# A feed-forward slab of two chunks, with its second products between the next slab's first products

## The chip, the cores and the metric

The kernel runs on one core of a Trainium2 chip. The metric is the device time of one execution in microseconds. A profile of one execution gives the span from the first to the last instruction and what each engine did in it: TensorE (PE for matmuls, PEld for loading their weights), VectorE (DVE), ScalarE (ACT), GpSimd (POOL) and SyncE (SP), which issues nearly all transfers from memory.

## The reference

The kernel computes one decoder layer in float32 on 256 tokens of 2048 channels: a SwiGLU feed-forward part, a token mixer, a second feed-forward part and a last normalization.

```
def swiglu(h, w_in, w_out):
    gu = h @ w_in
    gate, up = gu[..., :D_FF], gu[..., D_FF:]
    return (jax.nn.silu(gate) * up) @ w_out

# h = h + 1/2 * SwiGLU_1(RMSNorm(h))
# u = RMSNorm(h) @ W_in_mix, pooling heads and gated linear attention on parts of u
# h = h + concat(y_pool, y_gla) @ W_out_mix
# h = h + 1/2 * SwiGLU_2(RMSNorm(h))
# output = RMSNorm_final(h)
```

D_FF is 5632, so that a feed-forward part multiplies 256 x 2048 by 2048 x 11264 (the first product, gate and up) and 256 x 5632 by 5632 x 2048 (the second product).

## The kernel before, in words

**Numbers.** Each float32 operand is split into a rounded part hi and a remainder lo, and a product is three matmuls of 128x512: hi by hi, hi by lo, lo by hi (`three`, L165). Weights arrive raw, 1 MB a step (`load`, L101, three buffers). ScalarE writes hi (L108), VectorE writes lo (L109), into tiles of 128x1024 from a pool `units` of 14.

**Steps.** A step multiplies a 2 x 2 block of activations (two token tiles, two channel tiles of 128) by a 2 x 2 block of weights (two channel tiles, two column blocks of 512). In kind S that is 8 products (24 matmuls, `Group.s`). In kind W it is 7 (21 matmuls, `Group.w`), in the manner of Winograd: VectorE makes differences of weight blocks (`w_step`, L147, L151, L153), their splits follow, and the activations come with four sums S1 to S4 (`s_sums`, L342, split like the rest). Two of the results of W steps gather in tiles of their own (pw) and are put together by `combine` (L271 on ScalarE, L272 to L275 on VectorE); the result goes to the other accumulators by L428 in a first product and to h by L473 in a second product.

**Stages.** The first product goes in 11 chunks of 512 columns of gate and up, 8 steps each. A chunk of kind PLAIN has 8 S steps, one of MIXED 4 S and 4 W steps. After a chunk ScalarE takes silu (L435), VectorE multiplies by up (fa, L437), TensorE transposes (ftp, L444, eight of 128x128), and hi and lo of the result (fhi L449, flo L450) are the activations of the second product. Chunks are gathered in slabs of 4, 4 and 3. When the chunks of a slab are done, its second product runs in two halves of 1024 output columns, with 8 or 6 steps (table OUT), and is added to h with a factor 0.5 (`to_h`, L473; in the last slab of the first feed-forward part `finish1`, L592, which goes on to the transposes tp_h and splits h_hi, h_lo, L290, that the mixer needs). Names: fi and zi are first products of the first and second part, fo and zo second products; fo8_0 is half 0 of the slab that begins with chunk 8; wl_fo1_19 is a lo tile of half 1, step 19.

**Order.** The program is written as one list; a scheduler sets the order on each engine from it, and each engine runs its own list in order. x comes transposed in pairs of channel tiles (`x_act`, L530), is scaled and split within chunk 0, and for four of the eight pairs the sums S1 to S4 are made at the same place. The tiles for them, for fa and for raw x come from a pool `tmp` with two buffers of tag "act". Accumulators and pw tiles use two groups of PSUM banks, x and y, that change places with each product.

## Time and profile before

| | |
|---|---|
| median of 3 runs | 1734.99 us (1734.27 to 1735.23) |
| the profiled execution | 1734.83 us |
| its span | 1733.1 us |
| granted TensorE clock, mean over the span | 0.997 |
| busy share: TensorE, VectorE, ScalarE | 99%, 76%, 53% |
| read from memory | 334.56 MB, 194 GB/s over the span |

Times in the profile are in microseconds from the span's start unless marked ns. A matmul's duration in a list is longer than its pace, since matmuls overlap; the pace is read from starts, or from how long a row of them takes in the chain of waits. In the same way instructions of one engine that follow each other overlap by a little: a row "x4" of a timeline runs from the first's start to the last's end. A bracket "[0.77 <-DVE wl_fo L109]" is the time that the engine was idle before the row, and who ended it. What lies around the span in the profiled execution is 1.7 us.

### The profile page before, as it was taken

How to read it: one execution, taken by the hardware profiler on the slowest of the kernel's cores; microseconds unless marked ns; L12 is line 12 of the kernel's file. 1: busy time of each engine (PE TensorE's matmuls, PEld its weight loads, DVE VectorE, ACT ScalarE, POOL GpSimd, SP SyncE). 2: the span in 40 equal slices, each digit the busy share in tenths (PEclk: the TensorE clock that was granted, in tenths of full speed). 3: DMA queues.
4: the chain of work that ended last, by engine and by line, in shares of the span. 5: the costliest groups of instructions: out<-in, count | busy, mean ns of one | idle time of the engine just before them, and what ended most of it. 6: DMA issues, size and time to landing. Idle time of an engine off the chain costs nothing.

```text
span 1733.1 us, 20485 instructions
## 1 busy us (share of the span) xinstructions
PE 1717.8 (99%) x7840; PEld 1427.4 (82%) x7840; DVE 1316.3 (76%) x1493; ACT 911.1 (53%) x1117; POOL 24.9 (1%) x23
## 2 busy tenths in 40 slices
...
GB/s 344 189 230 169 194 235 194 189 199 187 201 210 182 215 196 148 211 183 140 200 212 146 191 176 168 224 165 194 201 236 167 222 165 200 217 219 150 252 189 91
DMA packets 52340, 337.98 MB, mean 195 GB/s; under 512 B 6017, under 2 KB 9217, under 8 KB 13330
## 3 DMA queue, kind: packets, MB, share of 16 engines
...
q8 instruction: 61, 1.00, 0.2%
...
HBM read 334.56 MB, written 2.10 MB: 194 GB/s over the span
## 4 chain that ended last, share of the span: by engine, by line
PE 97%; DMA 1%; ACT 1%; DVE 1%; issue 0%; SPq 0%; DVEq 0%; POOLq 0%; POOL 0%; ACTq 0%
PE ps_zi L165 24%; PE ps_fi L165 22%; PE ps_fo L165 11%; PE ps_zo L165 11%; PE ps_h L165 5%; PE pw_fi L165 3%; PE pw_zi L165 3%; PE ps_mp L165 3%; PE ps_mv L165 3%; PE pw_fo L165 2%; PE pw_zo L165 2%; PE ps_mg L165 2%; PE ps_mq L165 1%; PE ps_mk L165 1%; PE ps_mgr L165 1%; PE ftp L444 1%
## 5 line engine op out<-in xcount | busy, mean ns | idle before, releaser
L109 DVE TENSOR_TENSOR wl_zi<-wr_zi,wh_zi 128x1024 fp32r<-128x1024 f32 (+1 forms) x216 | 250.3, 1173 | 104.7 <-ACT wh_zi L108 98.1
L108 ACT CAST wh_zi<-wr_zi 128x1024 fp32r<-128x1024 f32 (+1 forms) x216 | 215.6, 1013 | 213.5 <-PE ps_zi L165 142.0
L109 DVE TENSOR_TENSOR wl_fi<-wr_fi,wh_fi 128x1024 fp32r<-128x1024 f32 (+1 forms) x218 | 249.8, 1163 | 85.7 <-ACT wh_fi L108 81.4
L108 ACT CAST wh_fi<-wr_fi 128x1024 fp32r<-128x1024 f32 (+1 forms) x218 | 214.4, 1004 | 189.5 <-PE ps_fi L165 116.5
L165 PE MATMUL ps_fi<-wh_fi,xT_hi 128*128 128x512 f32 x584 | 227.4, 391 | 1.7 <-ACT wh_fi L108 1.7
L165 PE MATMUL ps_fi<-wl_fi,xT_hi 128*128 128x512 f32 x584 | 228.4, 391 | 0.0
L165 PE MATMUL ps_zi<-wl_zi,h_hi 128*128 128x512 f32 x584 | 228.0, 390 | 0.0
L165 PE MATMUL ps_zi<-wh_zi,h_hi 128*128 128x512 f32 x584 | 227.9, 390 | 0.0
L165 PE MATMUL ps_zi<-wh_zi,h_lo 128*128 128x512 f32 x584 | 227.7, 390 | 0.0
L165 PE MATMUL ps_fi<-wh_fi,xT_lo 128*128 128x512 f32 x584 | 227.1, 391 | 0.1
L108 ACT CAST wh_zo<-wr_zo 128x1024 fp32r<-128x1024 f32 (+1 forms) x116 | 111.1, 999 | 96.9 <-DMA wr_zo<-in_ffn_w_out 34.0
L108 ACT CAST wh_fo<-wr_fo 128x1024 fp32r<-128x1024 f32 (+1 forms) x116 | 111.4, 999 | 94.4 <-DMA wr_fo<-in_ffn_w_out 34.8
L109 DVE TENSOR_TENSOR wl_fo<-wr_fo,wh_fo 128x1024 fp32r<-128x1024 f32 (+1 forms) x116 | 130.1, 1156 | 33.4 <-ACT wh_fo L108 33.1
L109 DVE TENSOR_TENSOR wl_zo<-wr_zo,wh_zo 128x1024 fp32r<-128x1024 f32 (+1 forms) x116 | 131.5, 1169 | 31.3 <-ACT wh_zo L108 30.9
L165 PEld LDWEIGHTS ps_fi<-wh_fi,xT_hi 128*128 128x128 f32 x584 | 110.0, 188 | 25.1 <-ACT wh_fi L108 2.6
L165 PEld LDWEIGHTS ps_fi<-wl_fi,xT_hi 128*128 128x128 f32 x584 | 110.1, 189 | 23.0 <-DVE wl_fi L109 0.4
L165 PEld LDWEIGHTS ps_fi<-wh_fi,xT_lo 128*128 128x128 f32 x584 | 109.9, 188 | 23.1 <-DVE xT_lo L290 0.5
L165 PEld LDWEIGHTS ps_zi<-wh_zi,h_lo 128*128 128x128 f32 x584 | 109.7, 188 | 22.5
L165 PEld LDWEIGHTS ps_zi<-wh_zi,h_hi 128*128 128x128 f32 x584 | 109.6, 188 | 22.4
L165 PEld LDWEIGHTS ps_zi<-wl_zi,h_hi 128*128 128x128 f32 x584 | 109.7, 188 | 22.3
L165 PE MATMUL ps_fo<-wl_fo,fhi 128*128 128x512 f32 x268 | 104.8, 391 | 0.8 <-DVE wl_fo L109 0.8
L165 PE MATMUL ps_zo<-wl_zo,zhi 128*128 128x512 f32 (+1 forms) x272 | 105.2, 387 | 0.0
...
## 6 DMA issues: line engine op xcount, KB each, us to landing
wr_zi<-in_ffn_w_in SPq DMA_DIRECT2D x88, 1024.0 KB, 5.0
wr_fi<-in_ffn_w_in SPq DMA_DIRECT2D x86, 1024.0 KB, 5.0
wr_fo<-in_ffn_w_out SPq DMA_DIRECT2D x44, 1024.0 KB, 5.0
wr_zo<-in_ffn_w_out SPq DMA_DIRECT2D x44, 1024.0 KB, 5.1
wr_h<-in_w_out_mix SPq DMA_DIRECT2D x16, 1024.0 KB, 4.9
wr_mv<-in_w_mv SPq DMA_DIRECT2D x8, 1024.0 KB, 4.8
wr_mp<-in_w_mp SPq DMA_DIRECT2D x8, 1024.0 KB, 4.9
...
```

What stands on the lines that cost most here:

```text
L108: nc.scalar.copy(out=hi, in_=src)
L109: nc.vector.tensor_tensor(out=lo, in0=src, in1=hi.bitcast(F32), op=ALU.subtract)
L165: nc.tensor.matmul(ps, x, y, start=start and i == 0, stop=stop and i == 2, **kw)
L444: nc.tensor.transpose(tp[:, t, k, :], a_t[t][:, k * P : (k + 1) * P], ident)
```

## The change

Slabs are of two chunks, the last of three. The second product of a slab is no longer behind its chunks: its half 0 stands behind the first chunk of the next slab, its half 1 behind the second. Only the last slab's second product stands at the end. The kinds of steps are listed by chunk: no W step in chunk 0, two in chunk 1, three in chunk 2, four in each of chunks 3 to 10; second products have S steps alone, but for two W steps in half 1 of the last slab. x is scaled and split in chunk 0 as before, but its sums S1 to S4 are made after chunk 0, from four pairs that are loaded again (`x_sums`). The tiles of the second product's activation sums go from three buffers to two. The loops of `ffn` become the functions `first_product` and `second_product`, called in the order of GROUPS.

```diff
-SLABS = ((0, 1, 2, 3), (4, 5, 6, 7), (8, 9, 10))
+SLABS = ((0, 1), (2, 3), (4, 5), (6, 7), (8, 9, 10))
...
-PLAIN = "SSSSSSSS"
-MIXED = "SWSWSWWS"
-MIXED_CHUNKS = (1, 3, 5, 7, 9)
+KINDS = (
+    "SSSSSSSS", "SSWSWSSS", "SSWSWWSS", "SWSWWWSS", "SWSWWWSS", "SWSWWWSS", "SWSWWWSS", "SWSWWWSS",
+    "SWSWWWSS", "SWSWWWSS", "SWSWWWSS",
+)
...
-    4: (
-        ((0, 0, "S"), (0, 1, "S"), (1, 0, "W"), (2, 0, "S"), (1, 1, "W"), (3, 0, "S"), (2, 1, "W"), (3, 1, "S")),
-        ((0, 0, "S"), (0, 1, "S"), (2, 0, "S"), (1, 0, "W"), (3, 0, "S"), (1, 1, "W"), (2, 1, "S"), (3, 1, "S")),
+    2: (
+        ((0, 0, "S"), (0, 1, "S"), (1, 0, "S"), (1, 1, "S")),
+        ((0, 0, "S"), (0, 1, "S"), (1, 0, "S"), (1, 1, "S")),
     ),
     3: (
-        ((0, 0, "S"), (0, 1, "S"), (1, 0, "W"), (2, 0, "S"), (1, 1, "W"), (2, 1, "S")),
+        ((0, 0, "S"), (0, 1, "S"), (1, 0, "S"), (1, 1, "S"), (2, 0, "S"), (2, 1, "S")),
         ((0, 0, "S"), (0, 1, "S"), (1, 0, "W"), (1, 1, "W"), (2, 0, "S"), (2, 1, "S")),
     ),
...
+GROUPS = (0, 1)
+for _s in range(1, len(SLABS)):
+    GROUPS += (SLABS[_s][0], (_s - 1, 0), SLABS[_s][1], (_s - 1, 1), *SLABS[_s][2:])
+GROUPS += ((len(SLABS) - 1, 0), (len(SLABS) - 1, 1))
...
+        for g in GROUPS:
+            if isinstance(g, int):
+                first_product(g)
+                continue
+            slab, ending = SLABS[g[0]], g[0] == len(SLABS) - 1
+            if ending and g[1] == 0 and behind is not None:
                 behind()
...
+            second_product(slab, g[1], ending)
...
-                if kp in W_PAIRS:
-                    nc.scalar.activation(out=f[:, j, :], in_=f[:, j, :], func=AF.Copy, scale=col)
-                else:
-                    scaled_split(hi[:, j, :], lo[:, j, :], f[:, j, :], col)
+                scaled_split(hi[:, j, :], lo[:, j, :], f[:, j, :], cols[j])
                 xT[2 * kp + j] = hi[:, j, :], lo[:, j, :]
-            if kp in W_PAIRS:
-                split_to(hi, lo, f)
-                x_s[kp] = s_factors(spool1, f, kp, "x")
         return xT[kt]
+
+    def x_sums():
+        for kp in W_PAIRS:
+            f, cols = x_pair(kp, "xs")
+            for j in range(2):
+                nc.scalar.activation(out=f[:, j, :], in_=f[:, j, :], func=AF.Copy, scale=cols[j])
+            x_s[kp] = s_factors(spool1, f, kp, "x")
```

In the kernel after, the lines named above have other numbers: L109 is L116, L147 L154, L151 L158, L153 L160, L272 to L275 L279 to L282, L165 L172, L428 L437, L437 L446, L444 L453, L473 L483, L592 L614, L342 L349, L290 L297.

VectorE at the end of a second product, in the first feed-forward part, before: half 1 of the first slab (fo0_1) and the splits of the next first product's plain chunk (fi4) around it.

```order
L272 TENSOR_TENSOR add_fo0_1_1_2092<-pw_fo0_1_0_1992,add_fo0_1_0_2091 128x512
L109 TENSOR_TENSOR wl_fi4_1_0_2209<-wr_fi4_1_2206,wh_fi4_1_0_2208 128x1024
L273 TENSOR_TENSOR add_fo0_1_0_2091<-pw_fo0_1_1_1993,add_fo0_1_1_2092 128x512
L274 TENSOR_TENSOR add_fo0_1_1_2092<-pw_fo0_1_1_1993,add_fo0_1_1_2092 128x512
L473 SCALAR_TENSOR_TENSOR h0_76<-add_fo0_1_0_2091,h0_76 128x1024
L109 TENSOR_TENSOR wl_fi4_1_1_2213<-wr_fi4_1_2206,wh_fi4_1_1_2212 128x1024
L275 TENSOR_TENSOR add_fo0_1_1_2092<-pw_fo0_1_1_1993,add_fo0_1_1_2092 128x512
L109 TENSOR_TENSOR wl_fi4_2_0_2243<-wr_fi4_2_2240,wh_fi4_2_0_2242 128x1024
L473 SCALAR_TENSOR_TENSOR h1_77<-add_fo0_1_1_2092,h1_77 128x1024
L473 SCALAR_TENSOR_TENSOR h0_76<-ps_fo0_1_0_1867,h0_76 128x1024
L473 SCALAR_TENSOR_TENSOR h1_77<-ps_fo0_1_1_1868,h1_77 128x1024
```

The same place after, at the end of half 0 of the second slab (fo2_0), with the splits of chunk 5 (fi5), whose pairs 1, 3, 4 and 6 are W steps.

```order
L116 TENSOR_TENSOR wl_fi5_3_0_2435<-wr_fi5_3_2432,wh_fi5_3_0_2434 128x512
L154 TENSOR_TENSOR wr_fi5_3_2432<-wr_fi5_3_2432 128x1024
L116 TENSOR_TENSOR wl_fi5_1_3_2372<-wr_fi5_1_2354,wh_fi5_1_3_2371 128x1024
L483 SCALAR_TENSOR_TENSOR h0_76<-ps_fo2_0_0_2178,h0_76 128x1024
L483 SCALAR_TENSOR_TENSOR h1_77<-ps_fo2_0_1_2179,h1_77 128x1024
L116 TENSOR_TENSOR wl_fi5_2_0_2401<-wr_fi5_2_2398,wh_fi5_2_0_2400 128x1024
L116 TENSOR_TENSOR wl_fi5_2_1_2405<-wr_fi5_2_2398,wh_fi5_2_1_2404 128x1024
L116 TENSOR_TENSOR wl_fi5_3_1_2439<-wr_fi5_3_2432,wh_fi5_3_1_2438 128x1024
L158 TENSOR_TENSOR wr_fi5_3_2432<-wr_fi5_3_2432 128x512
L160 TENSOR_TENSOR wr_fi5_3_2432<-wr_fi5_3_2432 128x512
L116 TENSOR_TENSOR wl_fi5_3_2_2445<-wr_fi5_3_2432,wh_fi5_3_2_2444 128x1024
L116 TENSOR_TENSOR wl_fi5_3_3_2450<-wr_fi5_3_2432,wh_fi5_3_3_2449 128x1024
```

The combine of a second product and two of its four additions to h are gone; two additions stand among the splits and differences of a W chunk, and this comes eight times in a feed-forward part where it came four times.

TensorE in chunk 1 before: where the transposes of chunk 0's result (ftp0) stand.

```order
L165 MATMUL ps_fi1_1_547<-wh_fi1_0_1_554,xT_lo0_113 128x512
L444 MATMUL ftp0_531<-ident_80,fa0_0_525 128x128 x4
L165 MATMUL ps_fi1_1_547<-wh_fi1_0_1_554,xT_hi0_109 128x512
...
L165 MATMUL ps_fi1_0_546<-wh_fi1_2_0_628,xT_hi1_110 128x512
L444 MATMUL ftp0_531<-ident_80,fa0_1_529 128x128 x4
L165 MATMUL pw_fi1_0_603<-wh_fi1_1_0_584,xT_hi0_109 128x512
```

The same after, in chunk 1 still, but behind the first matmuls of the second W step (pair 3).

```order
L172 MATMUL ps_fi1_0_562<-wh_fi1_3_1_716,shi_x_3_509 128x512
L172 MATMUL ps_fi1_0_562<-wl_fi1_3_1_717,shi_x_3_509 128x512
L172 MATMUL ps_fi1_0_562<-wh_fi1_3_1_716,slo_x_3_510 128x512
L453 MATMUL ftp0_547<-ident_80,fa0_0_541 128x128 x4
L172 MATMUL ps_fi1_1_563<-wh_fi1_3_3_727,xT_hi1_110 128x512
...
L453 MATMUL ftp0_547<-ident_80,fa0_1_545 128x128 x4
L172 MATMUL pw_fi1_0_653<-wh_fi1_1_0_634,xT_hi0_109 128x512
```

The transposes moved from a place in chunk 1's first step to one in its fifth.

VectorE at the end of the first feed-forward part's half 0 of the last slab (fo8_0) before, with the splits for half 1 (fo1).

```order
L273 TENSOR_TENSOR add_fo8_0_0_5237<-pw_fo8_0_1_5139,add_fo8_0_1_5238 128x512
L274 TENSOR_TENSOR add_fo8_0_1_5238<-pw_fo8_0_1_5139,add_fo8_0_1_5238 128x512
L151 TENSOR_TENSOR wr_fo1_18_5398<-wr_fo1_18_5398 128x512
L147 TENSOR_TENSOR wr_fo1_19_5442<-wr_fo1_19_5442 128x1024
L473 SCALAR_TENSOR_TENSOR h0_76<-add_fo8_0_0_5237,h0_76 128x1024
L109 TENSOR_TENSOR wl_fo1_18_2_5411<-wr_fo1_18_5398,wh_fo1_18_2_5410 128x1024
L275 TENSOR_TENSOR add_fo8_0_1_5238<-pw_fo8_0_1_5139,add_fo8_0_1_5238 128x512
L153 TENSOR_TENSOR wr_fo1_18_5398<-wr_fo1_18_5398 128x512
L592 SCALAR_TENSOR_TENSOR h0_76<-ps_fo8_0_0_5047,h0_76 128x512 x2
L473 SCALAR_TENSOR_TENSOR h1_77<-add_fo8_0_1_5238,h1_77 128x1024
L109 TENSOR_TENSOR wl_fo1_18_3_5416<-wr_fo1_18_5398,wh_fo1_18_3_5415 128x1024
L592 SCALAR_TENSOR_TENSOR h1_77<-ps_fo8_0_1_5048,h1_77 128x512 x2
```

The same place after.

```order
L154 TENSOR_TENSOR wr_fo1_19_5448<-wr_fo1_19_5448 128x1024
L116 TENSOR_TENSOR wl_fo1_18_1_5411<-wr_fo1_18_5404,wh_fo1_18_1_5410 128x1024
L158 TENSOR_TENSOR wr_fo1_18_5404<-wr_fo1_18_5404 128x512
L160 TENSOR_TENSOR wr_fo1_18_5404<-wr_fo1_18_5404 128x512
L614 SCALAR_TENSOR_TENSOR h0_76<-ps_fo8_0_0_5080,h0_76 128x512 x2
L614 SCALAR_TENSOR_TENSOR h1_77<-ps_fo8_0_1_5081,h1_77 128x512 x2
L116 TENSOR_TENSOR wl_fo1_18_2_5417<-wr_fo1_18_5404,wh_fo1_18_2_5416 128x1024
L116 TENSOR_TENSOR wl_fo1_18_3_5422<-wr_fo1_18_5404,wh_fo1_18_3_5421 128x1024
L116 TENSOR_TENSOR wl_fo1_19_1_5455<-wr_fo1_19_5448,wh_fo1_19_1_5454 128x1024
```

The combine of half 0 and its two additions L473 are gone from between the splits; the four L592, now L614, stand together.

## Rows read from the trace of the kernel before

**Rows 1.** The page: busy time of each engine with its share of the span and its instructions, and the shares of the chain that ended last by engine.

```profile
PE 1717.8 (99%) x7840; PEld 1427.4 (82%) x7840; DVE 1316.3 (76%) x1493; ACT 911.1 (53%) x1117; POOL 24.9 (1%) x23
...
PE 97%; DMA 1%; ACT 1%; DVE 1%; issue 0%; SPq 0%; DVEq 0%; POOLq 0%; POOL 0%; ACTq 0%
```

**Rows 2.** The waits of TensorE: what waited for what, us in total, times, the longest.

```profile
PE ps_fi L165 <- ACT wh_fi L108: 1.7, 1, 1.7
PE idle L519 <- DVE zeros L516: 1.2, 1, 1.2
PE ps_fo L165 <- DVE wl_fo L109: 0.8, 1, 0.8
PE ps_mgr L165 <- ACT h_hi L289: 0.4, 1, 0.4
PE ps_fo L165 <- ACT wh_fo L108: 0.4, 1, 0.4
PE ps_mgr L165 <- DVE h_lo L290: 0.2, 1, 0.2
```

**Rows 3.** The chain that ended last, three pieces of it: start, us, what.

```profile
36.86 20.47 PE ps_fi L165 x89
...
265.13 46.92 PE ps_fi L165 x207
...
329.34 7.48 PE ps_fi L165 x33
```

**Rows 4.** Stretches of the span: from and to, their length, then busy time and instructions of PE, PEld, DVE, ACT and POOL, the granted TensorE clock, the share of DMA, GB/s. They are the start, 10 us around the end of chunk 0, a plain chunk (4), a mixed chunk (5), both halves of the second slab's second product, and the place of the waits in Rows 2 at a second product (the end of the first feed-forward part).

```profile
0.00:11.00 11.00, 8.14 (x21) 4.36 (x22) 4.18 (x10) 5.44 (x10) 0.69 (x6) 0.87 0.76 237
...
50.00:60.00 10.00, 10.00 (x48) 8.26 (x47) 9.30 (x11) 7.85 (x9) 0.00 (x0) 1.00 0.39 117
...
265.10:308.30 43.20, 43.20 (x193) 35.76 (x192) 26.44 (x24) 18.34 (x20) 0.00 (x0) 1.00 0.52 179
308.30:350.30 42.00, 42.00 (x191) 34.77 (x190) 34.77 (x37) 23.87 (x27) 0.00 (x0) 1.00 0.60 216
436.60:521.20 84.60, 84.60 (x379) 70.10 (x378) 75.50 (x78) 43.89 (x48) 0.00 (x0) 1.00 0.57 201
690.00:705.00 15.00, 13.88 (x67) 10.94 (x67) 13.61 (x18) 10.54 (x21) 0.00 (x0) 1.00 0.42 130
```

**Rows 5.** TensorE in the order of time, 698 to 702 us: start, us to the end, what, and the idle time before it.

```profile
698.02 0.39 PE L165 MATMUL ps_fo<-wh_fo,fsolo 128*128 128x512 f32 x1
698.76 0.49 PE L165 MATMUL ps_fo<-wh_fo,fhi 128*128 128x512 f32 x1 [0.35 <-ACT wh_fo L108]
700.02 0.50 PE L165 MATMUL ps_fo<-wl_fo,fhi 128*128 128x512 f32 x1 [0.77 <-DVE wl_fo L109]
...
701.05 1.03 PE L370 MATMUL tp_h<-ident,h 128*128 128x128 f32 x8
701.94 0.50 PE L165 MATMUL ps_fo<-wl_fo,fhi 128*128 128x512 f32 x1
```

**Rows 6.** VectorE in the order of time, ahead of that place.

```profile
679.43 0.68 DVE L272 TENSOR_TENSOR add_fo<-pw_fo,add_fo 128x512 f32<-128x512 f32 x1
...
684.70 1.22 DVE L473 SCALAR_TENSOR_TENSOR h<-add_fo,h 128x1024 f32<-128x1024 f32 x1
685.84 1.22 DVE L109 TENSOR_TENSOR wl_fo<-wr_fo,wh_fo 128x1024 fp32r<-128x1024 f32 x1
...
688.17 1.28 DVE L592 SCALAR_TENSOR_TENSOR h<-ps_fo,h 128x512 f32<-128x512 f32 x2
...
698.74 1.22 DVE L109 TENSOR_TENSOR wl_fo<-wr_fo,wh_fo 128x1024 fp32r<-128x1024 f32 x1 [0.45 <-ACT wh_fo L108]
```

**Rows 7.** TensorE in the order of time in chunk 0.

```profile
36.35 0.39 PE L165 MATMUL ps_fi<-wl_fi,xT_hi 128*128 128x512 f32 x1
36.86 0.50 PE L165 MATMUL ps_fi<-wh_fi,xT_lo 128*128 128x512 f32 x1
```

**Rows 8.** The page's transfers: issuer, number, KB each, median us from issue to landing (the weights of first products, and the pairs of x).

```profile
wr_fi<-in_ffn_w_in SPq DMA_DIRECT2D x86, 1024.0 KB, 5.0
...
xr<-in_xT SPq DMA_DIRECT2D x8, 256.0 KB, 6.9
```

**Rows 9.** VectorE's groups by line and shape, 265.13 to 521.21 us (the second slab's four chunks and its second product): instructions, busy us and mean ns of one, idle time before them and who ended it.

```profile
L109 DVE TENSOR_TENSOR wl_fi<-wr_fi,wh_fi 128x1024 fp32r<-128x1024 f32 x72 | 87.1, 1223 | 35.9 <-ACT wh_fi L108 34.1 <-PE ps_fi L165 1.2
...
L437 DVE SCALAR_TENSOR_TENSOR fa<-ps_fi,rx_r,fs 128x512 f32<-128x512 f32 x8 | 6.0, 746 | 1.7 <-ACT fs L435 1.7
...
L109 DVE TENSOR_TENSOR wl_fi<-wr_fi,wh_fi 128x512 fp32r<-128x512 f32 x8 | 5.5, 688 | 0.9 <-ACT wh_fi L108 0.9
...
L342 DVE TENSOR_TENSOR sf_f<-sf_f,ftp 128x128 f32<-128x128 f32 x3 | 0.9, 285 | 0.1
```

**Rows 10.** VectorE in the order of time, where instructions follow each other without a pause.

```profile
66.12 4.62 DVE L109 TENSOR_TENSOR wl_fi<-wr_fi,wh_fi 128x1024 fp32r<-128x1024 f32 x4
...
433.94 0.68 DVE L273 TENSOR_TENSOR add_fi<-pw_fi,add_fi 128x512 f32<-128x512 f32 x1
434.54 0.68 DVE L274 TENSOR_TENSOR add_fi<-pw_fi,add_fi 128x512 f32<-128x512 f32 x1
...
445.00 0.74 DVE L437 SCALAR_TENSOR_TENSOR fa<-ps_fi,rx_r,fs 128x512 f32<-128x512 f32 x1
445.66 5.76 DVE L109 TENSOR_TENSOR wl_fo<-wr_fo,wh_fo 128x1024 fp32r<-128x1024 f32 x5
```

**Rows 11.** VectorE's splits of the first tiles of a second product, and the chain's piece with which it begins on TensorE.

```profile
426.47 2.35 DVE L109 TENSOR_TENSOR wl_fo<-wr_fo,wh_fo 128x1024 fp32r<-128x1024 f32 x2
...
436.64 11.79 PE ps_fo L165 x52
```

**Rows 12.** ScalarE's largest group in the stretch of Rows 9, with who ended the idle time before it.

```profile
L108 ACT CAST wh_fi<-wr_fi 128x1024 fp32r<-128x1024 f32 x73 | 75.8, 1052 | 79.1 <-PE ps_fi L165 53.6 <-PE ps_fo L165 8.6 <-DVE wr_fi L153 6.9
```

**Rows 13.** TensorE in the order of time at the start of chunk 0.

```profile
8.68 0.63 PE L165 MATMUL ps_fi<-wh_fi,xT_hi 128*128 128x512 f32 x1
9.11 0.63 PE L165 MATMUL ps_fi<-wl_fi,xT_hi 128*128 128x512 f32 x1
```

More of the change, by code (lines that the diff above doesn't have):

```diff
@@ L384, in transposed_rows, with ffn @@
                 scaled_split(hi[:, kk, :], lo[:, kk, :], tp[:, k, :], cols[kk])
-    def ffn(psum, spool, act, s_in, w_in, w_out, row, name, finish, first=False, behind=None):
+    def ffn(psum, spool, act, s_in, w_in, w_out, row, name, finish, first=None, behind=None):
         turn = [0 if first else 1]
@@ L524, in layer, with x_pair @@
     x_hi, x_lo = new_hT("xT")
+    def x_pair(kp, name):
+        f = tmp.tile([P, 2, T], F32, tag="act", name=f"{name}{kp}")
+        nc.sync.dma_start(
+            out=f,
+            in_=io["xT"][kp * 2 * P : (kp + 1) * 2 * P, :].rearrange("(k p) t -> p k t", p=P),
+        )
+        return f, [gains[:, 0, 2 * kp + j : 2 * kp + j + 1] for j in range(2)]
     def x_act(kt):
```

201 lines of the change are left out of this document (98 added, 103 removed).

## The prediction

> **What bounds the kernel now.** I read the page's busy shares and its chain first [rows 1]: TensorE is busy in 99% of the span and 97% of the chain that ended last is TensorE's, so the time is, to a few microseconds, the number of matmuls times their pace. Second, the waits of TensorE [rows 2]: 4.7 us in the whole run, of which 0.8 + 0.4 us are in second products and the rest at the start or in the mixer. Third, the chain of waits in order of time, for the pace [rows 3]: 33 matmuls in 7.48 us, which is 0.2267 us each; the reader checks it on 207 in 46.92 (0.2267) and 89 in 20.47 (0.2300, with a pause in it). Fourth, stretches of one stage each [rows 4], for the engine that comes next: VectorE works 26.44 of 43.20 us in a chunk of eight-product steps alone, 34.77 of 42.00 in one with four seven-product (W) steps, and 75.50 of 84.60 us (89%) in a second-product stage, with TensorE busy in all of it. VectorE is what stands behind TensorE, and the change gives it more to do in the first products.
>
> **Term 1, fewer matmuls: -6.80 us.** A step of eight products (S) is 8 x 3 = 24 matmuls, a W step 7 x 3 = 21. W steps before, in each of the two feed-forward parts: 5 mixed chunks x 4 = 20 in first products; in second products, by the table OUT, 3 and 2 in the halves of each slab of four (10) and 2 and 2 in the last slab (4): 34, so 68 in all. After: 2 + 3 + 8 x 4 = 37 in first products and 2 in one second product: 39, so 78. Ten more, 30 matmuls fewer, which is also the difference of TensorE's rows in the two orders (7631 and 7601). All are 128x512 and on the path: 30 x 0.2267 = 6.80 us.
> The Trainium skill (TensorE: Matmul & The Clock Gate, "Wait — 56ns, not 53.3ns?") gives 512/2.4 GHz + about 2.5 ns = 215.7 ns for such a matmul at full clock; with it this term would be 6.47 us. The rows show 226.7 ns, and the measurement decides.
>
> **Term 2, the stall at the end of the first part's second products: -1.55 us.** [rows 5] show TensorE's starts there: 698.02 to 698.76 and 698.76 to 700.02, 0.74 and 1.26 us where 0.2267 is the pace, so 1.55 us lost to one hi and one lo tile. [rows 6] show what VectorE had in front of that lo tile since 679.43: four instructions that combine the W products of half 0 (L272 to L275, start to start 0.60 us, 2.4 us), two L473 that add that to h (2 x 1.14), and the extra sums and splits of W steps. After, half 0 of the last slab has no W step: combine and its L473 are gone (4.7 us), and of each W step that turns S the half-width split, L147, L151, L153 and one wide split (2 x 1.13 + 3 x 0.60 = 4.1 us), 8.2 for two. That is 12.9 us of VectorE's work taken from in front of a tile that was 1.3 us late. The order of after also has four L614 that wait for half 0's last matmul in front of splits of half 1; those splits are first wanted two S steps (48 matmuls, 10.9 us) later, and three wide instructions and four of about 0.6 us end some 6 us after it. So nothing is late next, and I count all 1.55. If the cover is thinner than this the term is 0.
>
> **Term 3, the start: -0.28 us.** [rows 7]: in chunk 0 one matmul starts 0.51 us after the one before it, 0.28 over the pace, behind a lo tile of x on an engine that also makes the W sums of x. These sums leave chunk 0, so I count 0.28.
>
> **Term 4, the sums of x after chunk 0: +0.5 us.** x_sums loads four pairs again (4 x 256 KB on SP's queue, 6.9 us from issue to landing each [rows 8]; SP's queue is in front of the weights of chunk 1, and DMA is 39% busy in 50 to 60 us [rows 4], so four of them fit), scales them on ScalarE and gives VectorE 16 small sums and 4 half-width splits: 16 x 0.285 + 4 x 0.69 = 7.3 us by listed durations [rows 9], now between the splits of chunk 1's W steps. VectorE then works without a pause for 25 us or more, and the last tiles it makes there (the second transposes' source, fa0_1, and the split wl_fi1_3_3) are wanted when they are ready to within half a microsecond. The transposes of chunk 0 stand 87 matmuls after its last one where they stood 18 after, 19.7 us instead of 4.1, which is the scheduler's answer to that. Bounds: 0 (as all of it ran hidden in chunk 0) and 7.3 us (all of it in the open). The nearest row is the stage with VectorE at 89% and no wait, so I take 0.5.
>
> **Term 5, VectorE in the steady cycle: 0.** A first product with four W steps and the S-only second product behind it are 180 + 96 = 276 matmuls and 8 transposes: 62.6 + 0.9 us (eight transposes take 0.89 from the first's start to the next matmul [rows 5]), 63.5 us. VectorE has 36 wide instructions in it (per W step two splits, the split of T and L154, per S step two splits, two adds of the combined products, two L483), 18 half-width ones, and 2 of L446. Listed durations [rows 9] give 36 x 1.223 + 18 x 0.688 + 2 x 0.746 = 57.9 us, 91%. But instructions that follow each other overlap [rows 10]: four wide ones take 4.62 us, (4.62 - 1.22)/3 = 1.13 us each, and narrow ones start every 0.60, so it is 36 x 1.13 + 18 x 0.60 + 2 x 0.66 = 52.8 us, 83%. Within the first product alone it is 41.5 us (26 wide, 18 narrow, 2) against 41.7 of TensorE: level, no reserve; the reserve is made up in the second product (10 wide ones, 11.3 us, against 21.8).
> The tight place is the three W steps in a row. L483 waits for the last matmul of the second product and everything behind it on VectorE waits too. From there to the split of the S step after the three W steps are 16 wide and 8 narrow ones, 22.9 us (25.1 by listed durations); TensorE comes to it after 132 matmuls, 29.9 us. So VectorE is 5 to 7 us ahead there. Before, leads went from 9 us at the start of a second product (a lo tile done at 427.69, used at 436.64 [rows 11]) to almost none at 698, and only the latter cost anything. Bounds: 0 a chunk, and 45.6 - 41.7 = 3.9 us a chunk where nothing overlaps and no reserve is carried in, x 16 chunks = 62. The nearest row is again the second-product stage of before: 89% by the same listed durations and no wait. I take 0.
>
> Moving the second products costs nothing by itself: same loads of 1 MB, 5.0 us each [rows 8], in another order; the queue of weights is limited by free tiles, not by DMA (ScalarE's casts wait 53.6 us for TensorE to free one in that stretch [rows 12]).
>
> **Sum.** -6.80 - 1.55 - 0.28 + 0.5 + 0 = -8.1 us. The profiled execution took 1734.83 us, span 1733.1 and 1.7 around it; after: 1726.7. The median of three runs is 1734.99, 0.16 above; I predict 1726.8.
>
> **Rivals.**
> *Only the matmuls count.* The 1.55 us stay, or come back as another wait of that size (x_sums at 2 us, a late tile at the end of a part). For it: VectorE's rows grow slightly and its pauses are used up; against it: 12.9 us less in front of the late tile. -6.8 to -4.8: 1728.2 to 1730.2.
> *VectorE falls behind in the W chunks, slower.* The mechanism is the run of three W steps: VectorE makes 6.4 us of work for each (4 x 1.13 + 3 x 0.60) while TensorE uses it up in 21 x 0.2267 = 4.76, so the lead falls by 1.6 us a step, and it starts late since L483 holds the queue. For it: 41.5 against 41.7 us leaves nothing for VectorE's own waits on ScalarE's casts, and 16 chunks follow each other. Against: mixed chunks before had 34.77 busy in 42.00 without a wait, and the second product between refills the lead. It decides from 8.1/16 = 0.51 us a chunk on, where all the gain is gone; with 1.0 us each it is 1726.8 + 16 = 1743, with 3.9 each 1789.
> Stalls of 1 us are no longer than those of [rows 5], in whose stretch the granted clock was 1.00, the full 2.4 GHz [rows 4], so I count no slower clock with them. What the lower level costs is seen at the start, after TensorE had waited for its first weights: matmuls start every 0.43 us [rows 13] in a stretch with a mean clock of 0.87, 0.2 us a matmul more; a chunk whose stall brought that on for ten matmuls would pay 2 us more, 32 us over 16. The Trainium skill (TensorE: Matmul & The Clock Gate, "What's actually happening") says that an idle array goes back to 1.2 GHz. For a stall of 1.5 us rows 4 speak against it, so that case is the far end of this rival, 1775, and has 0.01 of its chance.
> *It ends level.* Ten W steps give 6.8 us and the chunks take about that back, 0.3 to 0.6 us each: 1731.5 to 1738.5.
>
> **How the numbers follow.** The forecast (1724.5 to 1728.5) has 0.68, only the matmuls 0.13, level 0.08, VectorE behind 0.11. A difference under 0.2%, 3.5 us, can't be told from none. Forecast and first rival are faster than 1731.5: 0.81; level 0.08; slower 0.11. The range goes from 1724.0 (no x_sums cost, and a little less waiting in the mixer's start) to 1732.0, which holds the first two and the edge of the third; the long tail above is left out.
>
> **What would show it.** 7810 matmuls on the page instead of 7840; TensorE's waits below 4 us, with none at second products; DVE at 78 to 80% of the span; in any cycle of 63.5 us no wait of TensorE and VectorE's busy time at 55 to 58; between 52 and 75 us a wait of at most 1 us at ftp or at a wl_fi tile. It is wrong if waits for wl_fi tiles (L116) stand in every chunk from 3 on, in the third W step or the S step behind it, or if the pace of matmuls changes.

## The result and the profile after

| | before | after |
|---|---|---|
| median | 1734.93 us (4 runs, 1734.27 to 1735.23) | 1724.91 us (4 runs, 1724.72 to 1725.12) |
| the profiled execution | 1734.83 us | 1725.05 us |
| its span | 1733.1 us | 1723.2 us |
| granted TensorE clock, mean | 0.997 | 0.998 |

The ratio is 0.9943, with a 95% interval of 0.9926 to 0.996: 10.0 us faster, where 8.1 were forecast. Between the profiled executions it is 9.78 us, and the accounts below are made on these.

The page of the kernel after: busy time, share of the span and instructions of each engine, and the chain that ended last.

```profile
PE 1709.8 (99%) x7810; PEld 1422.3 (83%) x7810; DVE 1363.9 (79%) x1503; ACT 919.7 (53%) x1117; POOL 22.1 (1%) x23
...
PE 99%; issue 0%; ACT 0%; DVE 0%; DMA 0%; DVEq 0%; POOLq 0%; POOL 0%; ACTq 0%
```

Against [rows 1]: 30 matmuls fewer, VectorE 47.6 us busier, the chain 99% TensorE's where it was 97%. The waits of TensorE after, in the columns of [rows 2]:

```profile
PE ps_fi L172 <- ACT wh_fi L115: 1.8, 1, 1.8
PE idle L536 <- DVE zeros L533: 1.2, 1, 1.2
PE ps_mgr L172 <- ACT h_hi L296: 0.4, 1, 0.4
PE ps_mgr L172 <- DVE h_lo L297: 0.2, 1, 0.2
```

The two waits at a second product (ps_fo) are gone, and none has come. Stretches after, in the columns of [rows 4]: from 11 to 60 us, chunk 1 and the first second product's beginning, a cycle in the middle of the first part, and the place where the stall of [rows 5] had been.

```profile
11.00:60.00 49.00, 49.00 (x217) 40.56 (x217) 36.06 (x53) 37.20 (x63) 0.71 (x1) 1.00 0.85 324
60.00:104.00 44.00, 44.00 (x199) 36.43 (x198) 41.58 (x53) 26.48 (x32) 0.00 (x0) 1.00 0.60 200
399.20:462.70 63.50, 63.50 (x286) 52.58 (x285) 55.33 (x57) 33.67 (x37) 0.00 (x0) 1.00 0.57 199
684.00:699.00 15.00, 15.00 (x76) 12.53 (x75) 11.83 (x16) 8.46 (x13) 0.00 (x0) 1.00 0.47 159
```

TensorE is busy all the time in each. The cycle (a first product with four W steps and the half second product behind it) is 63.5 us long, as counted, with 55.33 us of VectorE (87%, the second product included). How far VectorE is ahead at the tightest place is read from two timelines. First VectorE's, in the three W steps of chunk 7 on end, with the two pauses that it makes there:

```profile
430.26 3.07 DVE L116 TENSOR_TENSOR wl_fi<-wr_fi,wh_fi 128x1024 fp32r<-128x1024 f32 x3 [1.19 <-ACT wh_fi L115]
...
435.96 7.05 DVE L116 TENSOR_TENSOR wl_fi<-wr_fi,wh_fi 128x1024 fp32r<-128x1024 f32 x6
444.66 1.23 DVE L116 TENSOR_TENSOR wl_fo<-wr_fo,wh_fo 128x1024 fp32r<-128x1024 f32 x1 [1.65 <-PE ps_fi L172]
```

Then TensorE's first use of the first of those six tiles, the T tile of the third W step:

```profile
442.21 0.39 PE L172 MATMUL pw_fi<-wl_fi,shi_x 128*128 128x512 f32 x1
```

The first of the six ends about 1.2 us after the start of the group, at 437.2, and is used at 442.21: a lead of 5.0 us. Behind the group VectorE itself waits 1.65 us for TensorE to free a tile: it has caught up. The same lead comes in each cycle of chunks 3 to 9 to a few hundredths. In chunk 1, behind the sums of x, the lead is far smaller. VectorE's last split there, then TensorE's first use of its tile:

```profile
71.35 1.22 DVE L116 TENSOR_TENSOR wl_fi<-wr_fi,wh_fi 128x1024 fp32r<-128x1024 f32 x1
```

```profile
72.70 0.42 PE L172 MATMUL ps_fi<-wl_fi,xT_hi 128*128 128x512 f32 x1
```

It ends at 72.57, 0.13 us ahead.

One thing that the prediction had no term for is the end of the kernel. The last additions to h in VectorE's timeline and the last power on GpSimd, before and after (L921 is L943, L958 is L980 in the kernel after). Before:

```profile
1719.23 1.29 DVE L921 SCALAR_TENSOR_TENSOR h<-ps_zo,h 128x512 f32<-128x512 f32 x2 [0.89 <-PE ps_zo L165]
...
1722.24 0.28 PE L165 MATMUL ps_zo<-wh_zo,zlo 128*128 128x256 f32 x1
...
1726.16 0.56 POOL L958 TENSOR_TENSOR fin_r<-fin_v,neg_half 128x1 f32<-128x1 f32 x1 [3.77 <-DVE fin_v L954]
```

After:

```profile
1707.90 1.29 DVE L943 SCALAR_TENSOR_TENSOR h<-ps_zo,h 128x512 f32<-128x512 f32 x2 [0.49 <-PE ps_zo L172]
...
1713.17 0.28 PE L172 MATMUL ps_zo<-wh_zo,zlo 128*128 128x256 f32 x1
...
1716.05 0.56 POOL L980 TENSOR_TENSOR fin_r<-fin_v,neg_half 128x1 f32<-128x1 f32 x1 [5.00 <-DVE fin_v L976]
```

Before, the first token tile's accumulators were ready 3.0 us ahead of the last matmul, after, 5.3 us. Its normalization is then done while TensorE still works, and the second tile's power starts 2.88 us after the start of the last matmul, not 3.92. From the start of the last matmul to the end of the span it is 10.1 us where it was 10.8: some 0.75 us of the gain.

### The profile page after: what moved, and what is told of

Its sections match the earlier page's. It is cut to its first block, busy times and chain, and to the rows that moved or that the text cites. A ratio compares the mean times of both kernels' runs of the same rounds, so it can differ in the third digit from the quotient of the medians.

```text
span 1723.2 us, 20490 instructions
## 1 busy us (share of the span) xinstructions
PE 1709.8 (99%) x7810; PEld 1422.3 (83%) x7810; DVE 1363.9 (79%) x1503; ACT 919.7 (53%) x1117; POOL 22.1 (1%) x23
## 4 chain that ended last, share of the span: by engine, by line
PE 99%; issue 0%; ACT 0%; DVE 0%; DMA 0%; DVEq 0%; POOLq 0%; POOL 0%; ACTq 0%
PE ps_fi L172 21%; PE ps_zi L172 20%; PE ps_fo L172 14%; PE ps_zo L172 13%; PE pw_fi L172 6%; PE pw_zi L172 6%; PE ps_h L172 5%; PE ps_mp L172 3%; PE ps_mv L172 3%; PE ps_mg L172 2%; PE ps_mq L172 1%; PE ps_mk L172 1%; PE ps_mgr L172 1%; PE ztp L453 1%; PE ftp L453 1%; PE tp_h L377 0%
## 5 line engine op out<-in xcount | busy, mean ns | idle before, releaser
L116 DVE TENSOR_TENSOR wl_zi<-wr_zi,wh_zi 128x1024 fp32r<-128x1024 f32 (+1 forms) x250 | 280.0, 1143 | 59.0 <-ACT wh_zi L115 52.0
L116 DVE TENSOR_TENSOR wl_fi<-wr_fi,wh_fi 128x1024 fp32r<-128x1024 f32 (+1 forms) x252 | 279.2, 1134 | 39.4 <-ACT wh_fi L115 34.1
L172 PE MATMUL ps_fi<-wl_fi,xT_hi 128*128 128x512 f32 x482 | 187.9, 391 | 0.0
L172 PE MATMUL ps_fi<-wh_fi,xT_hi 128*128 128x512 f32 x482 | 186.1, 392 | 1.8 <-ACT wh_fi L115 1.8
L172 PE MATMUL ps_zi<-wh_zi,h_lo 128*128 128x512 f32 x482 | 187.7, 390 | 0.0
L172 PE MATMUL ps_zi<-wl_zi,h_hi 128*128 128x512 f32 x482 | 187.6, 389 | 0.0
L172 PE MATMUL ps_zi<-wh_zi,h_hi 128*128 128x512 f32 x482 | 187.3, 390 | 0.0
L172 PE MATMUL ps_fi<-wh_fi,xT_lo 128*128 128x512 f32 x482 | 187.1, 390 | 0.0
L116 DVE TENSOR_TENSOR wl_fo<-wr_fo,wh_fo 128x1024 fp32r<-128x1024 f32 (+1 forms) x92 | 110.0, 1207 | 30.2 <-ACT wh_fo L115 26.8
L172 PE MATMUL ps_zo<-wh_zo,zlo 128*128 128x512 f32 (+1 forms) x344 | 133.9, 389 | 0.0
L172 PE MATMUL ps_zo<-wl_zo,zhi 128*128 128x512 f32 (+1 forms) x344 | 133.8, 389 | 0.0
L172 PE MATMUL ps_fo<-wh_fo,flo 128*128 128x512 f32 x340 | 133.4, 392 | 0.0
L172 PE MATMUL ps_zo<-wh_zo,zhi 128*128 128x512 f32 (+1 forms) x344 | 133.3, 387 | 0.0
L172 PE MATMUL ps_fo<-wl_fo,fhi 128*128 128x512 f32 x340 | 133.2, 392 | 0.0
L172 PE MATMUL ps_fo<-wh_fo,fhi 128*128 128x512 f32 x340 | 132.1, 390 | 0.0
L116 DVE TENSOR_TENSOR wl_zo<-wr_zo,wh_zo 128x1024 fp32r<-128x1024 f32 (+1 forms) x92 | 112.6, 1235 | 22.4 <-ACT wh_zo L115 21.8
L172 PEld LDWEIGHTS ps_fi<-wh_fi,xT_hi 128*128 128x128 f32 x482 | 90.9, 189 | 21.4 <-ACT wh_fi L115 2.7
L172 PEld LDWEIGHTS ps_fi<-wl_fi,xT_hi 128*128 128x128 f32 x482 | 90.9, 189 | 19.2 <-DVE wl_fi L116 0.2
```

Of the source, the lines that this page charges most:

```text
L116: nc.vector.tensor_tensor(out=lo, in0=src, in1=hi.bitcast(F32), op=ALU.subtract)
L172: nc.tensor.matmul(ps, x, y, start=start and i == 0, stop=stop and i == 2, **kw)
```

## The experiments

Theory: the time is TensorE's matmuls at 0.2267 us; the ten W steps, the stall at the end of the first part, and the late start in chunk 0 make the gain, and VectorE's load costs nothing because each second product refills the lead that the first one uses up. Rivals: the gain is not the W steps' but the order's; VectorE's load in the W chunks costs something already; the place of the second products does not matter. Each run stands beside runs of the kernel before on the same chip, whose medians were 1734.6 to 1734.8; the changed kernel's 1724.9 stood beside 1734.9, so a few tenths of a difference to it may lie outside the edit.

**As many W steps as before.**

```diff
-    "SSSSSSSS", "SSWSWSSS", "SSWSWWSS", "SWSWWWSS", "SWSWWWSS", "SWSWWWSS", "SWSWWWSS", "SWSWWWSS",
-    "SWSWWWSS", "SWSWWWSS", "SWSWWWSS",
+    "SSSSSSSS", "SSWSWSSS", "SSWSWWSS", "SWSWWWSS", "SWSWWWSS", "SWSWWWSS", "SSWSWWSS", "SSWSWWSS",
+    "SSWSWWSS", "SSWSWWSS", "SSWSWWSS",
```

> The changed kernel with five W steps fewer in each feed-forward part (chunks 6 to 10 have three instead of four), so 68 as before the change, and everything else as in the changed kernel: 30 matmuls more. If each W step is worth its three matmuls and nothing else (TensorE is the path): 1724.9 + 30 x 0.2267 = 1731.7, within 0.4, and the page counts 7840 matmuls. If VectorE's load in the chunks with four W steps had cost something that the trace does not show as a wait, less than 1731. Against the kernel before, with as many matmuls, it should stand at -3.2: that part of the gain is then not W steps.

Measured: 1732.01 us (ratio 0.9985, 0.9975 to 0.9994); the profiled execution 1731.97, 6.92 over that of the changed kernel, for 30 matmuls at 0.231 us. So the W steps are worth their matmuls, VectorE's load in the W chunks takes nothing from them, and some 2.6 to 2.9 us of the gain are something else (3.2 were expected).

**W steps back in half 0 of the last slab.**

```diff
-        ((0, 0, "S"), (0, 1, "S"), (1, 0, "S"), (1, 1, "S"), (2, 0, "S"), (2, 1, "S")),
+        ((0, 0, "S"), (0, 1, "S"), (1, 0, "W"), (2, 0, "S"), (1, 1, "W"), (2, 1, "S")),
```

> The changed kernel with the two W steps put back in half 0 of the last slab's second product, in both parts: 12 matmuls fewer, -2.72. If the combine of half 0 and its additions to h in front of half 1's splits made the stall at the end of the first part, TensorE's two late starts (about 1.5 us, and some 0.3 in the matmuls behind them) come back there, and the end of the kernel grows by about 0.8 again: 1724.9 - 2.7 + 1.8 + 0.8 = 1724.8. If the stall had another cause (the old slabs of four): 1722.2, and no wait of TensorE for wl_fo near the end of the first part.

Measured: 1732.91 us (ratio 0.999, 0.9981 to 0.9999), 8.0 over the changed kernel although it has 12 matmuls fewer. The waits of TensorE at second products came back, in both parts:

```profile
PE ps_fo L172 <- ACT wh_fo L115: 1.6, 2, 1.0
PE ps_fo L172 <- DVE wl_fo L116: 1.5, 2, 0.8
...
PE pw_zo L172 <- ACT wh_zo L115: 1.0, 1, 1.0
PE ps_zo L172 <- DVE wl_zo L116: 0.7, 1, 0.7
PE tp_h L377 <- DVE h_lo L297: 0.5, 2, 0.4
```

They are at the place of the old stall, twice:

```profile
692.36 0.51 PE L172 MATMUL ps_fo<-wh_fo,fhi 128*128 128x512 f32 x1 [0.60 <-ACT wh_fo L115]
693.62 0.51 PE L172 MATMUL ps_fo<-wl_fo,fhi 128*128 128x512 f32 x1 [0.76 <-DVE wl_fo L116]
...
697.82 0.50 PE L172 MATMUL ps_fo<-wh_fo,fhi 128*128 128x512 f32 x1 [0.95 <-ACT wh_fo L115]
699.08 0.68 PE L172 MATMUL ps_fo<-wl_fo,fhi 128*128 128x512 f32 x1 [0.76 <-DVE wl_fo L116]
```

So half 0's W steps make this stall, but the expected size was wrong: 10.7 us (8.0 + 12 x 0.2267) where 2.6 were expected. By TensorE's starts in the profiled execution (10.9 us there) some 6.9 us are at the end of the first part, 3.3 at the end of the second, which had no wait there before, and 1.0 behind the last matmul; the start was some 0.3 us faster. Part of the first is the clock, though no wait in this stretch was longer than 0.95 us: behind the four waits above eight starts are 0.43 to 0.47 us apart (699.55 to 702.54 us), some 1.6 us more than at the pace. The stretch in the columns of [rows 4]:

```profile
699.00:703.00 4.00, 3.92 (x10) 3.11 (x11) 4.00 (x7) 2.69 (x4) 0.00 (x0) 0.57 0.54 172
```

Behind the two waits of [rows 5] the clock had stayed at 1.00. Before the change the chunk ahead of the last second product, chunk 10, was plain and left VectorE a reserve; now it has four W steps. That the plain chunk 10 kept the stall small is inferred: no run has W steps in half 0 and a plain chunk 10 in the new order. If so, the two halves of the change need each other: W steps could go into chunk 10 because they left half 0.

**The sums of x in chunk 0 again.** The splitting of x is as before the change, and `x_sums` does nothing.

```diff
     def x_sums():
-        for kp in W_PAIRS:
...
+        pass
```

> The changed kernel with the sums of x made in chunk 0 again, as before the change, and no second load of four pairs. If these sums made the late start at 36.35 us of the kernel before: it comes back in chunk 0, 0.3 to 0.4 us, and chunk 1 runs as in the changed kernel or easier: 1725.2 to 1725.4. If the sums behind chunk 0 cost something there (a wait at the transposes ftp0): that goes, up to -0.3: 1724.6 to 1725.0.

Measured: 1725.62 us (ratio 0.9945, 0.9931 to 0.996), the profiled execution 1725.54, 0.49 over that of the changed kernel. In chunk 0 one start comes 0.84 us after the one before it (41.86 us), 0.62 over the pace; chunk 1 is no faster. The end of the kernel is 0.3 us shorter in this execution, so the total shows less than the starts. The first reading held, with 0.6 us for the 0.3 to 0.4 expected: the sums cost time in chunk 0 and none behind it.

**The second products not between.**

```diff
-    GROUPS += (SLABS[_s][0], (_s - 1, 0), SLABS[_s][1], (_s - 1, 1), *SLABS[_s][2:])
+    GROUPS += ((_s - 1, 0), (_s - 1, 1), *SLABS[_s])
```

> The changed kernel with the second product of each slab of two behind its own two chunks, not between the next ones; the same steps and the same W steps. Two first products with four W steps then follow each other. VectorE has about 41.5 us of work for 41.7 of TensorE's in each. If that count (instructions overlapping, 1.13 us for a wide one) is right, the lead that VectorE brings holds over the two: within 1 us of 1724.9. If VectorE's work is nearer to the listed durations (45.6 us) the lead is used up in the second one and TensorE waits there 1 to 4 us in each of seven pairs: 1732 to 1753. Then the place between the chunks is what lets every chunk have four W steps.

Measured: 1751.64 us (ratio 1.0095, 1.008 to 1.011), 26.7 over the changed kernel, with the same work. The place between the chunks is what lets every chunk have four W steps. The starts of TensorE show where: about 1.5 us are lost in the second chunk of each pair of four W steps each (chunks 5, 7 and 9 of each part; chunk 3, behind a chunk with three W steps, loses nothing), and about 9 in chunk 10, the third on end. There, in the columns of [rows 4]:

```profile
600.00:620.00 20.00, 19.48 (x89) 15.68 (x89) 19.38 (x23) 11.00 (x14) 0.00 (x0) 1.00 0.50 178
620.00:640.00 20.00, 15.59 (x55) 11.21 (x54) 19.32 (x28) 9.93 (x14) 0.00 (x0) 0.87 0.50 170
640.00:660.00 20.00, 20.00 (x86) 16.45 (x85) 16.23 (x18) 11.32 (x12) 0.00 (x0) 0.96 0.71 254
```

VectorE works 97% of the first 40 us, and TensorE waits; behind its waits (one start 2.9 us after the one before it) the granted clock is 0.87 over 20 us, so part of that stretch ran at the lower of the two levels, 1.2 GHz. The Trainium skill (TensorE: Matmul & The Clock Gate, "What's actually happening") says that an array that stood idle goes back to it; the trace agrees, here, while after the shorter stall of [rows 5] the clock stayed at 1.00. In a pair it is less: the second chunk's waits come with VectorE and ScalarE waiting for each other in turn. ScalarE casts the T tiles of a W step once VectorE's last difference (L160) is made, and VectorE's next splits wait for those casts. ScalarE:

```profile
331.19 2.94 ACT L115 CAST wh_fi<-wr_fi 128x1024 fp32r<-128x1024 f32 x3 [3.62 <-DVE wr_fi L160]
337.20 2.95 ACT L115 CAST wh_fi<-wr_fi 128x1024 fp32r<-128x1024 f32 x3 [3.07 <-DVE wr_fi L160]
```

VectorE, in the same stretch:

```profile
332.26 3.50 DVE L116 TENSOR_TENSOR wl_fi<-wr_fi,wh_fi 128x1024 fp32r<-128x1024 f32 x3 [1.17 <-ACT wh_fi L115]
...
338.28 3.50 DVE L116 TENSOR_TENSOR wl_fi<-wr_fi,wh_fi 128x1024 fp32r<-128x1024 f32 x3 [1.19 <-ACT wh_fi L115]
```

So VectorE stands still for about 1.2 us behind the differences of a W step: a pause that the count of 41.5 us a first product left out. It comes at three of the four W steps of this chunk 5, and at one of four in the changed kernel's cycle (the row at 430.26), where the lead covers it.

**No W steps in half 0, in the kernel before.** The edit of half 0 of the changed kernel's OUT, in the kernel before: (1, 0) and (1, 1) are S, in the order of the changed kernel.

> The kernel before the change with half 0 of the last slab's second product of S steps alone, in both parts; all else as before the change. It has 12 matmuls more (+2.72). If the combine and the additions of half 0 are what made TensorE late at 698 us, those two waits (1.55 us, 1.85 with the matmuls behind them) are gone, and if they also set the order in which the last half's accumulators end, 0.8 at the end of the kernel: 1734.8 + 2.7 - 1.85 - 0.8 = 1734.9. If the waits had another cause they stay and it is 1737.5.

Measured: 1734.46 us (ratio 0.9999, 0.9989 to 1.0008) with 12 matmuls more. Its waits of TensorE are four, as in the changed kernel, none at a second product. So the stall is half 0's W steps' also by itself, and without it the old kernel stays where it was: those four W steps (two a part) cost what they saved. From the start of the last matmul to the end of the last instruction of an engine it takes 5.6 us; it is 6.4 before the change and with W steps back in half 0, and 5.3 in the changed kernel: the gain at the end, too, goes with half 0.

**One more instruction of VectorE in each W step, first try.**

```diff
+    spare = const.tile([P, 2, CW], F32, name="spare")
+    nc.gpsimd.memset(spare, 0.0)
...
+        nc.vector.tensor_tensor(out=spare, in0=spare, in1=spare, op=ALU.mult)
         t_hi, t_lo = split_pair(w[:, 0:2, :], f"{name}_2")
```

> The changed kernel with one more instruction of VectorE in each of the 78 W steps (128x1024 on a tile of its own, whose result nobody reads), 4.5 us more in a cycle of a first product with four W steps and the second product behind it. By overlapping durations VectorE then has 57.3 us of work in 63.5: if that is what counts, the lead of 5 to 7 us behind the three W steps shrinks to 0.5 to 2.5 and TensorE does not wait: 1725 to 1727. By listed durations it has 62.4 of 63.5, and the first product alone 50.1 in 41.7: TensorE waits 1 to 4 us in most of the 16 cycles, 1740 to 1785.

Measured: 1768.73 us (ratio 1.0195, 1.0175 to 1.0216). This run doesn't answer its question. The instruction reads nothing of the step, so the scheduler put all 78 into the first 300 us. The busy time of that tile's instructions alone, in two stretches:

```profile
0.00:300.00 300.00, 94.76 (x78) 0.97 0.54 187
300.00:1767.00 1467.00, 0.00 (x0) 1.00 0.56 193
```

The whole loss is there; behind it TensorE runs as in the changed kernel.

**The same, tied to its step.**

```diff
+        nc.vector.tensor_tensor(out=spare, in0=w[:, 0:2, :], in1=w[:, 0:2, :], op=ALU.mult)
         t_hi, t_lo = split_pair(w[:, 0:2, :], f"{name}_2")
```

> The changed kernel with one more instruction of VectorE in each W step, as before, but one that reads that step's raw weights, so that it can't be moved ahead of the step (its result is read by nobody). VectorE has 4.5 us more in each cycle of 63.5 and 3.4 more in the three W steps in a row, where its lead was 5.0 us in the changed kernel's trace. If the second product gives the lead back: no wait of TensorE in the cycles of chunks 3 to 9, waits of 2 to 3 us in chunk 1 (lead there 0.1) and of 1 to 3 us in chunk 10 of each part (lead there 2.3): 1729 to 1734. If the lead drifts down from cycle to cycle: waits in most cycles, 1740 and more.

Measured: 1728.44 us (ratio 0.9963, 0.9947 to 0.9978), 3.5 over the changed kernel, and 63 of the 78 instructions behind 300 us. Two cycles of the first part and one of the second, in the columns of [rows 4]:

```profile
335.70:399.20 63.50, 63.50 (x285) 52.56 (x284) 59.20 (x61) 33.40 (x37) 0.00 (x0) 1.00 0.57 203
399.20:462.70 63.50, 63.50 (x285) 52.59 (x284) 57.92 (x61) 33.38 (x37) 0.00 (x0) 1.00 0.56 195
...
1253.50:1317.00 63.50, 63.50 (x286) 52.59 (x285) 60.21 (x62) 34.44 (x38) 0.00 (x0) 1.00 0.56 199
```

A cycle bears four or five instructions more, 4.5 us or more by their starts: 63.5 us as before, with VectorE at 91 to 95%, and no wait. What it costs is at the two places that the expectation names from the changed kernel's leads: 1.0 us in chunk 1 (a start 0.93 us after the one before it, and slow ones behind) and 1.3 in chunk 10 of the first part; the rest, about 1.1, is in the first 14 us, where the matmuls kept the slow pace of [rows 13] until 13.0 us instead of 10.6. In the second part there is no wait, and the one expected in its chunk 10 did not come.

**Five W steps in chunks 3 to 10.**

```diff
-W_PAIRS = (1, 3, 4, 6)
+W_PAIRS = (1, 3, 4, 6, 7)
...
-    "SSSSSSSS", "SSWSWSSS", "SSWSWWSS", "SWSWWWSS", ...
+    "SSSSSSSS", "SSWSWSSS", "SSWSWWSS", "SWWSWWWS", ...
```

> The changed kernel with five W steps and three S steps in chunks 3 to 10 (pair 7 gets sums too): 16 W steps more, 48 matmuls fewer, -10.9. VectorE has 4.1 us more in each cycle (56.9 of 62.8 by overlapping durations, 91%), and 45.6 in a first product of 41.0. If the second product gives back what the first takes: 1714 to 1715. If the first product's 4.6 us too much is not covered by the lead: TensorE waits up to 4 us in each of 16, against 10.9 gained: 1725 to 1775, with the clock lower in the longer waits.

Measured: 1730.19 us (ratio 0.9977, 0.9967 to 0.9987; ten runs, 1728.5 to 1735.5): 5.3 over the changed kernel with 48 matmuls fewer, so 16 us of waits and of what follows them, 1 us a chunk in the mean. They begin at chunk 6 of the first part (383 us) and chunk 5 of the second (1319 us) and are longest in chunk 10, and most of them are waits for ScalarE's hi tiles, with the pauses between the engines that are described above. A cycle of chunk 8 in the first part, in the columns of [rows 4]:

```profile
455.60:518.40 62.80, 62.33 (x277) 50.86 (x276) 56.83 (x61) 33.52 (x39) 0.00 (x0) 1.00 0.57 197
```

VectorE is at 90% here and TensorE waits; with the tied instruction it was at 91 to 95% and TensorE did not. So the busy share alone does not say whether a cycle fits. VectorE's waits for the casts of the first product's tiles differ the other way: 6.0 us between 393 and 456 us in this run, 3.4 us between 399 and 463 us in the tied one.

**More W steps at the start of the second part.** There the sums are ready before chunk 0.

```diff
+KINDS2 = ("SSWSWWSS", "SSWSWWSS", "SWSWWWSS")
...
-            kinds = KINDS[c]
+            kinds = KINDS2[c] if name == "z" and c < 3 else KINDS[c]
```

> The changed kernel with five W steps more in the second feed-forward part, where the sums of the activations are ready before chunk 0: three in chunk 0, three in chunk 1 and four in chunk 2, instead of none, two and three. 15 matmuls fewer, -3.4. Chunks 0 and 1 follow each other without a second product between them. If VectorE keeps its lead over two chunks of three W steps: 1721.3 to 1721.8. If not, TensorE waits in chunk 1, as in the pairs of the run with the second products behind their slabs (1.1 us each): 1722.4, and up to 1726 if the mixer's end leaves VectorE late.

Measured: 1722.26 us (ratio 0.9927, 0.9912 to 0.9942), 2.65 under the changed kernel, where the 15 matmuls alone are 3.4 and 3.1 or more were expected; no new wait in the list, but some 0.5 us of slow starts in chunk 2. Here too chunks 0, 1 and 2 follow each other; with three, three and four W steps that costs little. With four in each of the three chunks (the string "SWSWWWSS" three times):

> The changed kernel with four W steps in each of chunks 0, 1 and 2 of the second feed-forward part instead of none, two and three: 21 matmuls fewer, -4.8. Chunks 0 and 1 have no second product between them. If a pair of chunks with four W steps costs what it did with the second products behind their slabs (1.1 to 1.7 us): 1721.3 to 1721.9. If VectorE's lead holds over this one pair: 1720.2. Much longer waits, 1724 and more, would mean that the end of the mixer leaves no lead at all.

Measured: 1727.84 us (ratio 0.996, 0.9945 to 0.9975): 2.9 over the changed kernel with 21 matmuls fewer, so 7.7 us of waits, five times what was expected. The expectation spoke of a pair, but the order of GROUPS (0, 1, 2, then the first second product) puts three chunks on end there, as in the last slab of the run with the second products not between, where three cost 1.5 + 9 us. The list of waits shows them at hi tiles:

```profile
PE pw_zi L174 <- ACT wh_zi L117: 2.1, 4, 0.7
...
PE ps_zi L174 <- ACT wh_zi L117: 0.9, 4, 0.2
PE pw_zi L174 <- DVE wl_zi L118: 0.4, 2, 0.2
```

They stand in chunk 1 (1060 to 1085 us) and in chunk 2 (1106 to 1131 us).

**The two together, and five W steps where there is room.** Kinds of the second part's first chunks as in the 3-3-4 run, five W steps in chunks 3, 4 and 5 of both parts, pair 7 with sums.

> The changed kernel with three, three and four W steps in the first chunks of the second part (-15 matmuls, 1722.3 measured) and five W steps in chunks 3, 4 and 5 of both parts (-18 matmuls, -4.1). In the run with five everywhere TensorE did not wait before chunk 6 of the first part. If the lead is spent only over several such cycles: 1718.2, with up to 0.5 for the fifth sum of x in chunk 1. If each chunk with five W steps costs about 1 us, as the mean over all 16 did: 1722 to 1724.

Measured: 1720.47 us (ratio 0.9918, 0.9903 to 0.9933), the fastest version, 4.4 under the changed kernel where 6.7 were expected. The first part lost some 0.8 us in chunk 1, which makes the fifth sum, and 0.2 in chunks 3 to 5; the second part lost 2 us in chunk 5 alone (1313 to 1320 us). Why its chunk 5 does and the first part's does not stays open.

**Four buffers of raw weights, with the second products not between.**

```diff
-RAW_BUFS = 3
+RAW_BUFS = 4
...
-MIX_BLOCKS = 10
+MIX_BLOCKS = 9
...
-                a21 = ftmp[0].tile([P, P], F32, tag="a21", name=f"a21_{name}{c}_{pr}")
+                a21 = tmp.tile([P, CW], F32, tag="sil", name=f"a21_{name}{c}_{pr}")[:, :P]
```

> The kernel with each slab's second product behind its own chunks (1751.6 us), with four buffers of 1 MB for raw weights instead of three; to make room, one of ten mixer tiles is gone and a small copy of VectorE's sums lies in another pool (neither is part of the feed-forward chunks' work). If the waits of that kernel come from the supply (a W step holds its raw tile until VectorE's last difference and split, the next load of 5 us starts after that): most of its 26.7 us go, 1726 to 1735. If VectorE's amount of work in two and three chunks of four W steps on end sets them: 1747 to 1752.

Measured: 1749.86 us (ratio 1.0087, 1.0068 to 1.0107), 1.8 under the run with three, in the range of the second reading, with a part of the first in it. The pairs lose 1.0 us instead of 1.5 and chunk 10 about 7 instead of 9, some 6 us in all between the profiled executions, of which chunk 0 takes about 3.3 back with late starts behind 13, 24 and 37 us. So the supply has a small part in it. The rest goes with VectorE's work and its pauses for ScalarE, by the rows above; that they make it is not shown. Whether a shorter path between the two (another order of differences and casts, say) would remove the rest was not tried. The copy that was moved (a21) belongs to the activation sums of the last second product, made in the last slab, so the 2 us there may not be the fourth buffer's alone.

## Why the prediction was right

The direction, the forecast's own range and the wide one hold; the gain was 1.7 us larger than forecast, profiled execution against profiled execution, and the median lies 0.4 us inside the forecast's lower edge, 1724.5. The sum did not come near by errors that cancel: each term below came out as forecast or better. The signs that were named came too: 7810 matmuls, 3.6 us of waits with none at a second product, VectorE at 79%. By the terms of the sum, profiled execution against profiled execution:

| term | forecast | measured | from |
|---|---|---|---|
| 30 matmuls | -6.80 | -6.92 | as many W steps as before |
| stall at the end of the first part | -1.55 | -1.8 | trace after, and half 0 in both kernels |
| start | -0.28 | -0.33 | starts in chunk 0 |
| sums of x after chunk 0 | +0.5 | 0.0 | trace after, sums back in chunk 0 |
| VectorE in the cycle | 0 | 0 | trace after, one more tied instruction |
| end of the kernel | none | -0.75 | both traces |
| sum | -8.1 | -9.8 (9.78 measured) | |

- **What bounds it.** TensorE at 99% of the span and of the chain: right, and the matmul count carries seven tenths of the gain.
- **Term 2** was right in its place and its cause, as the two runs on half 0 show from both sides. It was too small by the matmuls behind the stall: [rows 5] show two starts, but two later ones are slow as well (700.02 to 700.36 and 701.94 to 702.27 us, 0.34 and 0.33 where 0.2267 is the pace), some 0.2 us together. The tile that the prediction calls 1.3 us late was 1.03 late (1.26 less the pace), which changes nothing in the sum. That nothing would be late next also held: 15.00 of 15.00 us busy at 684 to 699 us.
- **Term 3** came as counted: no late start between 11 and 60 us, 49.00 of 49.00 busy.
- **Term 4** had the margin right and the price wrong. The last split of chunk 1, wl_fi1_3_3, ended 0.13 us before its first use; the forecast said "to within half a microsecond" and took 0.5 us of stall for it, but a margin that is small and positive costs nothing. The run with the tied instruction shows how small it is: there chunk 1 does wait, and loses 1.0 us.
- **Term 5** was right in every number that it gave: a cycle of 63.5 us, a lead of 5 to 7 us at the S step behind the three W steps (5.1 measured there, 5.0 at the step before), VectorE's busy time at 55.3. Its count by starts was the right one, since 4.5 us more are borne. But "level, no reserve" for a first product by itself was too good: it left out that VectorE can stand still for 1.2 us behind a W step's differences until ScalarE's casts come. With a second product in between nothing is lost; without it 1.5 us are lost in a second chunk and 9 in a third. That the pauses make this loss is read from the timelines and was not tested by itself.
- **The missing term** is the end of the kernel. The prediction did not ask when the last half's accumulators are ready. The longer end goes with half 0's W steps: it is there in both runs that have them (6.4 us to the last instruction) and in neither of the two that compare without them (5.3 and 5.6).
- **The rivals.** "Only the matmuls count" fell with the stall. "VectorE falls behind" did not happen here, but its mechanism is real and near: the same W steps without second products between cost 26.7 us, and one W step more in every chunk costs more than it saves.
